# Output projection on normed operands, both parts summed in one bank; three units of up products in step; four reorders

## The chip, the cores and the metric

One core of one Trainium2 chip runs the program. The time is the device time of one execution in microseconds (us); the median of three runs is compared. All matrix products are done in split form: an operand is kept as a high part, rounded to the matmul's format, and a low part, the rest, and a product is three matmuls (high x high, high x low, low x high) into the same bank.

## What is computed

One layer of a hybrid encoder on 1024 tokens of width 1024: a shared norm and input projection, eight heads of attention beside a recurrent block (LRU), an output projection, a gated feed-forward layer of width 2816 with a causal convolution, and a gated addition at the end.

```python
hn = _rms_norm(x, g_mix[l])
proj = hn @ w_in[l]
cq, ckv, kr, xl, gl = jnp.split(proj, IN_SPLITS, axis=-1)
attn = _mla(cq, ckv, kr, positions, ...)
lru = _rglru_block(xl, gl, ...)
mixed = jnp.concatenate([_rms_norm(attn, g_attn_out[l]), _rms_norm(lru, g_lru_out[l])], axis=-1)
x = x + mixed @ w_out[l]
hf = _rms_norm(x, g_ffn[l])
up = _causal_dwconv(hf @ w_up[l], w_ffn_conv[l], b_ffn_conv[l])
gte, val = up[..., :D_FF], up[..., D_FF:]
x = x + (jax.nn.gelu(gte, approximate=True) * val) @ w_down[l]
gate = jax.nn.sigmoid(_rms_norm(x, g_ple[l]) @ w_ple_gate[l] + b_ple_gate[l])
x = x + gate * (p[l] @ w_ple[l])
```

`_rms_norm` divides each token by the root of its mean square and multiplies by a gain per channel.

## The kernel before

Activations lie transposed: 128 channels on the partitions, tokens along the row, in chunks `c` or `k` of 128 channels (eight of them for width 1024) and two halves `h` of 512 tokens. The program is one straight line of instructions. The functions lay down an order, each engine works through its own queue in order, and the tool that builds the program may put a ready instruction ahead of one that waits when it lays the queues down; semaphores are put in for it. DMAs are issued from SyncE's queue (SP), in order too. ScalarE makes high parts, VectorE low parts.

Stages, with their lines:

- `project` (L213) reads x, scales it by the gain, and sums its squares: ScalarE squares a chunk, and the sum over chunks (L255) is on GpSimd for odd chunks up to the fifth and on VectorE otherwise. The first two products run chunk by chunk as x comes in (L262).
- `lru` (L375) goes over four blocks of 128 channels. For each, two gates are computed by small products in the banks `bc` and `st` (L428, L430), then the recurrence; the result y is scaled by its gain, split (L455), and both parts go to DRAM. The sum of the squares of y (`yss`) is on ScalarE, GpSimd or VectorE by block (L460 to L464).
- `qkv` (L551) ends with a dummy Exp (L585) that loads ScalarE's table for the softmax. `attention` (L606) copies two mask rows into the operand buffers of both halves (L629, L633) and then runs jobs in an order by due times, in units of a twelfth of a head: `TURN_AT`, `PROBS_AT`, `BLOCK_AT`, `WEIGH_AT`, and `MIX_AT` for work on the output projection's operands. `mix_attn` (L828) scales a half chunk of the attention output by its gain, splits it, and squares it for the norm; `mix_lru` (L820) fetches the parts of y.
- `mix` (L746) is the output projection. For each half and output chunk, the lru part is summed in one bank and the attention part in another; each bank is multiplied by its norm's scale per token (`rl` and `r1`) and added to the residual `x1` (L773, L774, L786, L787). `measure` (L854) forms the norm's sums over channels on TensorE (L144), `scale` (L858) spreads the scale of each token over all partitions with two matmuls (L164). In the second half, the first operands of the next stage are made (`normed`, `operand`).
- `ffn` (L1019) computes the up products. A unit is 128 gate channels and 128 value channels; its four half-width products are formed from seven (numbered `p`), which need combined operands: B11 and B21 from the first half's residual, T1 to T4 and B22 from both. `T(n, k)` makes them on VectorE and ScalarE, `weights` and `finish_weights` make the combined weights, `product` runs the twelve matmuls, `sums` reads the banks `b1`, `b2`, `b3` into the output tiles `U`, and `finish_unit` (the epilogue, five steps) does convolution, GELU and product into tiles `u`. Units 0 and 1 run in step at the start, then one unit after another. The tiles `U` and `u` (four each) are opened after the residual tiles are closed.
- `down` (L1152) runs two halves of 22 steps of 24 matmuls; after each half `gained` makes the gate's operands and the squares of the new residual, whose sum is on GpSimd. `ple` (L1202) runs the gate's products; the scale of the first half is spread after the second product (n = 1), that of the second after the fifth (n = 4).

Of the kernel before, what the change touches and what calls it, by code (L numbers as in the profile page):

```python
# [47 lines left out]
MIX_AT = (4, 6, 7, 8)  # L48
# [26 lines left out]
class Block:  # L75
# [137 lines left out]
    def project(self):  # L213
# [22 lines left out]
        for k in range(NK):  # L236
# [13 lines left out]
            if k == 0:  # L250
                nc.scalar.activation(ssum, raw, AF.Square)
            else:
                sq = rp.tile([P, S], F32, tag="xsq", name="xsq", bufs=2)
                nc.scalar.activation(sq, raw, AF.Square)
                (nc.gpsimd if k % 2 and k < NK - 1 else nc.vector).tensor_tensor(out=ssum, in0=ssum, in1=sq, op=ALU.add)  # L255
# [119 lines left out]
    def lru(self, x, ws, done, then, scale):  # L375
# [43 lines left out]
        for c in range(NL):  # L419
# [3 lines left out]
            for j, b in ((0, "b_r"), (1, "b_i")):  # L423
                g = slice((2 * c + j) * P, (2 * c + j + 1) * P)
                o = L(b)
                for h in range(2):
# [26 lines left out]

            parts = bx.bitcast(F32R), m.bitcast(F32R)
# [96 lines left out]
    def qkv(self, t, c, uq, ukv):  # L551
# [31 lines left out]
        if t == NT - 1:  # L583

            nc.scalar.activation(tmp, tmp, AF.Exp, scale=0.0)  # L585
# [20 lines left out]
    def attention(self):  # L606
# [12 lines left out]
        self.e = []  # L619
# [6 lines left out]
        mask = self.w.tile([P, S], F32, tag="wraw", name="mask", bufs=3)  # L626
        nc.sync.dma_start(out=mask[QK:QK + NT], in_=self.i["mask"][0])
        for g in range(2):
            nc.scalar.copy(self.qb[g][0][QK:QK + NT], mask[QK:QK + NT, g * HALF:(g + 1) * HALF])  # L629
        mask = self.w.tile([P, S], F32, tag="wraw", name="mask", bufs=3)  # L630
        nc.sync.dma_start(out=mask[QK:QK + NT], in_=self.i["mask"][1])
        for g in range(2):
            nc.scalar.copy(self.kb[g][0][QK:QK + NT], mask[QK:QK + NT])  # L633
# [4 lines left out]
        jobs = []  # L638
# [8 lines left out]
        for at, f, args in zip(MIX_AT, (self.mix_attn, self.mix_attn, self.mix_lru, self.mix_attn), ((0, 0), (1, 0), (0,), (2, 0))):  # L647
# [10 lines left out]
        self.mix_attn(3, 0)  # L658
# [86 lines left out]

    def mix(self):  # L746
        nc = self.nc
        self.banks(at=3, lru=3, bc=1)
        self.c_x1, x1p = self.pool("x1", 1)
# [565 lines left out]
```

## Time and profile before

| what | value |
|---|---|
| median of three runs | 1244.38 us (1241.66 to 1244.45) |
| the profiled execution | 1244.59 us, span 1242.8 us |
| TensorE's mean granted clock | 0.984 |
| TensorE idle within the span | 41.5 us |
| HBM read, written | 97.36 MB, 28.31 MB |

The span is the time from the first to the last instruction of the profiled execution. PE is TensorE (PEld its weight loads), DVE VectorE, ACT ScalarE, POOL GpSimd, SP SyncE. A group of instructions is named by its line, engine, operation and tiles (`out<-in`). A line is often that of a helper: L108 is every chain of matmuls, L113 and L118 the low part of a split, L112 and L117 its high part.

Section 2 of the page cuts the span into forty slices; each digit is the busy share of a slice in tenths (9 is 90% or more), and PEclk is the granted clock in tenths of full speed:

```profile
PE   7999998999999998899999999999999998999998
PEclk9999998999999998899999999999999998999999
```

TensorE is busy nearly everywhere, and where a digit falls the clock's digit beside it often falls too.

### The profile page before, as it was taken

To read this page: it belongs to the slowest core of one execution; us is meant where nothing else is said; L and a number is where in the kernel's file an instruction comes from. 1 tells how busy PE (TensorE), PEld (TensorE's weight loads), DVE (VectorE), ACT (ScalarE), POOL (GpSimd) and SP (SyncE) were. 2 spreads that over 40 slices of the span, in tenths; PEclk is the share of its full clock that TensorE was granted. 3 is DMA by queue.
4 is the path that set the end of the run, shared out by engine and by line. 5 is a ranking of instruction groups with operands and counts; after the bars stand their busy time and mean duration, and the time that the engine had idled before them with its cause. 6 is when DMAs were issued, how large, how long until landed. Compare 5 with 4: busy or idle time off the path is not lost.

```text
span 1242.8 us, 15388 instructions
## 1 busy us (share of the span) xinstructions
PE 1201.3 (97%) x5600; PEld 1001.7 (81%) x5600; DVE 896.6 (72%) x1406; ACT 643.6 (52%) x1030; POOL 165.8 (13%) x180
## 2 busy tenths in 40 slices
PE   7999998999999998899999999999999998999998
PEld 5787986888878887788888888888888886888787
DVE  7879798777778699998878878778653346444633
ACT  7388677888874134654544545545432244333211
POOL 3012264444430000000000000000000021001200
PEclk9999998999999998899999999999999998999999
DMA  6213200111168220322222222122485336641221
GB/s 226 68 55 111 103 7 9 48 36 55 43 196 291 86 73 22 107 97 85 85 85 85 69 102 85 68 88 86 132 286 186 106 103 219 202 153 51 69 101 69
DMA packets 49932, 128.78 MB, mean 104 GB/s; under 512 B 5808, under 2 KB 8752, under 8 KB 49856
## 3 DMA queue, kind: packets, MB, share of 16 engines
q1 hardware_dynamic: 49856, 127.80, 30.2%
q8 instruction: 44, 0.72, 0.2%
q14 instruction: 32, 0.26, 0.1%
HBM read 97.36 MB, written 28.31 MB: 101 GB/s over the span
## 4 chain that ended last, share of the span: by engine, by line
PE 66%; DVE 6%; issue 1%; DMA 0%; ACT 0%; POOL 0%; POOLq 0%; DVEq 0%
PE b L108 31%; PE dn L108 16%; PE gt L108 6%; PE lru L108 4%; PE at L108 3%; PE st L108 2%; DVE m L118 1%; DVE B L911 1%; PE big L108 1%; DVE x L1038 1%; DVE x L1177 1%; DVE x L896 0%; PE p L734 0%; PE st L144 0%; DMA om<-oc 0%
## 5 line engine op out<-in xcount | busy, mean ns | idle before, releaser
L108 PE MATMUL b<-B,A 128*128 128x512 f32 x1848 | 424.9, 392 | 3.7 <-DVE U L992 3.4
L108 PEld LDWEIGHTS b<-B,A 128*128 128x128 f32 x1848 | 349.7, 190 | 78.0 <-issue 3.8
L108 PE MATMUL dn<-m,whi 128*128 128x512 f32 x616 | 191.9, 392 | 4.9 <-DVE m L113 4.9
L113 DVE TENSOR_TENSOR wlo<-wraw,whi 128x1024 fp32r<-128x1024 f32 (+2 forms) x59 | 68.1, 1157 | 123.8 <-ACT whi L112 123.8
L108 PEld LDWEIGHTS dn<-m,whi 128*128 128x128 f32 x616 | 116.8, 190 | 29.9 <-DVE m L113 5.4
L112 ACT CAST whi<-wraw 128x1024 fp32r<-128x1024 f32 (+2 forms) x59 | 58.4, 994 | 147.0 <-PE st L108 136.7
L108 PE MATMUL dn<-m,wlo 128*128 128x512 f32 x308 | 120.9, 392 | 0.0
L1004 DVE SCALAR_TENSOR_TENSOR u<-U,par,u 128x1023 f32<-128x1023 f32 x88 | 112.4, 1278 | 2.1 <-ACT u L1009 2.0
L846 POOL TENSOR_TENSOR ssum<-ssum,sq 128x512 f32<-128x512 f32 x14 | 21.4, 1532 | 658.7 <-ACT sq L842 657.9
L944 ACT CAST A<-s 128x512 fp32r<-128x512 f32 x88 | 54.7, 622 | 78.0 <-PE b L108 70.8
L108 PE MATMUL gt<-m,wh 128*128 128x512 f32 (+1 forms) x272 | 80.0, 377 | 0.0
L108 PE MATMUL big<-kT,qT 96*128 96x384 f32 (+11 forms) x288 | 68.7, 365 | 3.5 <-ACT kT L117 3.3
L952 DVE TENSOR_TENSOR A<-s,A 128x512 fp32r<-128x512 f32 x88 | 60.6, 689 | 14.7 <-ACT A L944 14.6
L108 PEld LDWEIGHTS dn<-m,wlo 128*128 128x128 f32 x308 | 58.5, 190 | 12.1
L972 ACT COPY keep<-b 128x512 f32<-128x512 f32 x66 | 38.4, 583 | 52.4 <-PE b L108 52.4
L702 DVE TENSOR_SCALAR_CACHE_REDUCE pr<-big,nrq 128x512 f32<-128x512 f32 (+3 forms) x64 | 51.9, 814 | 11.7 <-PE p L715 4.3
L706 POOL TENSOR_SCALAR pr<-pr,st 128x512 f32<-128x512 f32 (+3 forms) x64 | 48.2, 757 | 78.5 <-DVE st L705 59.9
L944 ACT CAST A<-wraw 128x512 fp32r<-128x512 f32 x54 | 33.4, 622 | 47.8 <-PE b L108 40.5
L108 PEld LDWEIGHTS big<-kT,qT 96*128 96x128 f32 (+1 forms) x288 | 50.3, 198 | 9.1 <-ACT kT L117 3.8
L108 PEld LDWEIGHTS gt<-m,wh 128*128 128x128 f32 x272 | 50.0, 188 | 9.3
L1009 ACT ACTIVATE u<-U,par 128x1024 f32<-128x1024 f32 x44 | 54.7, 1246 | 1.5 <-DVE U L994 0.4
L704 ACT ACTIVATE pr<-pr,st 128x512 f32<-128x512 f32 (+3 forms) x64 | 49.7, 777 | 8.0 <-DVE pr L702 6.8
(327 smaller groups left out, 2289.8 us busy)
## 6 DMA issues: line engine op xcount, KB each, us to landing
wraw<-w_down SPq DMA_DIRECT2D x44, 512.0 KB, 3.4
wraw<-w_up SPq DMA_DIRECT2D x33, 512.0 KB, 3.3
g<-u SPq DMA_DIRECT2D x22, 512.0 KB, 2.6
graw<-g SPq DMA_DIRECT2D x44, 256.0 KB, 4.1
raw<-w_up SPq DMA_DIRECT2D x11, 512.0 KB, 3.4
e<-eo SPq DMA_DIRECT2D x16, 256.0 KB, 2.4
m<-y SPq DMA_DIRECT2D x8, 512.0 KB, 7.2
x<-xT SPq DMA_DIRECT2D x16, 256.0 KB, 7.0
```

Of the source, the lines that this page charges most:

```text
L108: self.nc.tensor.matmul(out, lhsT=w, rhs=x, start=start and n == 0, stop=stop and n == len(terms) - 1, **kw)
L112: self.nc.scalar.copy(hi, src)
L113: (self.nc.gpsimd if pool else self.nc.vector).tensor_tensor(out=lo, in0=src, in1=hi.bitcast(F32), op=ALU.subtract)
L702: V.tensor_scalar(out=pv, in0=sc, scalar1=self.nrq[:, qt, h:h + 1], scalar2=None, op0=ALU.mult, op1=ALU.min, accum_out=st[:, 0:1])
L704: nc.scalar.activation(pv, pv, AF.Exp, bias=st[:, 0:1], scale=-1.0, accum_out=st[:, 1:2])
L706: nc.gpsimd.tensor_scalar(out=pr[:, :kend], in0=pr[:, :kend], scalar1=st[:, 2:3], scalar2=1.0, op0=ALU.mult, op1=ALU.mult)
L846: (nc.gpsimd if pool else nc.vector).tensor_tensor(out=self.ssum[key], in0=self.ssum[key], in1=sq, op=ALU.add)
L944: self.nc.scalar.copy(t[:, :HALF], src)
L952: self.nc.vector.tensor_tensor(out=lo, in0=src, in1=hi.bitcast(F32), op=ALU.subtract)
L972: self.nc.scalar.copy(t, self.bank[u, b])
L1004: tap = lambda z, d: V.scalar_tensor_tensor(out=self.u[u, z][:, d:], in0=self.U[u, z][:, :S - d], scalar=self.col(f"cw{2 - d}", z * NF + u ...
L1009: nc.scalar.activation(t, self.U[u, n], AF.Identity, bias=self.col("cb", n * NF + u), scale=self.col("cw2", n * NF + u))
```

## The change

In the output projection, the operands are normed before the matmuls. `scale_lru` spreads the lru norm's scale once, during the last head; `mix_lru` fetches y (now one tile, not two parts), multiplies it by gain and scale and splits it; `mix_attn` multiplies the attention output by gain and scale, after `measure` and `scale` of the attention norm, and splits it. The squares are a job of their own (`square_attn`). Both parts of a chunk are summed in one bank of seven; the order of parts in the first half is written out. One addition reads the bank into the residual.

The residual's sixteen half tiles are laid in eight whole ones with the tags `U` and `u`, which the up products' output tiles take over without the pool being closed. Units 0, 1 and 2 of the up products run in step at the start (units 0 and 1 before); T4 is made later; the raw weights rotate through five places in the order of w_up.

Reorders and smaller edits: all of the input's sums of squares on VectorE; the last block's second gate in one wide bank, with one Sigmoid; the sum of squares of y by ScalarE squares and VectorE additions; the dummy Exp and the second half's mask copies after the first two turns of head 0; the first half's `gained` spread over steps 1 to 8 of the down product's second half; the gate's scales spread after n = 2 and n = 5.

```diff
-                (nc.gpsimd if k % 2 and k < NK - 1 else nc.vector).tensor_tensor(out=ssum, in0=ssum, in1=sq, op=ALU.add)
+                nc.vector.tensor_tensor(out=ssum, in0=ssum, in1=sq, op=ALU.add)
...
+                if c == NL - 1 and j:
+                    ps = self.acc("big")
+                    for h in range(2):
+                        hs = slice(h * HALF, (h + 1) * HALF)
+                        self.chain(ps[:, hs], self.three(gw, (xch, xcl), (slice(None), g), (slice(None), hs)))
+                    nc.scalar.activation(o, ps, AF.Sigmoid, bias=self.col(b, c))
...
-            self.scaled(y, self.col("g_lru", c), *parts)
-            self.y.append(self.dr.tile([P, 2, S], F32, name=f"y{c}"))
-            for j, z in enumerate((bx, m)):
-                nc.sync.dma_start(out=self.y[c][:, j, :], in_=z)
+            self.y.append(self.dr.tile([P, S], F32, name=f"y{c}"))
+            nc.sync.dma_start(out=self.y[c], in_=y)
...
-                e = V if c == NL - 1 else nc.gpsimd
-                e.tensor_tensor(out=gl, in0=y, in1=y, op=ALU.mult)
-                e.tensor_tensor(out=self.yss, in0=self.yss, in1=gl, op=ALU.add)
+                nc.scalar.activation(gl, y, AF.Square)
+                V.tensor_tensor(out=self.yss, in0=self.yss, in1=gl, op=ALU.add)
...
-            nc.scalar.activation(tmp, tmp, AF.Exp, scale=0.0)
...
+        hide(0)
...
+        jobs = [(TURN_AT[0] + .1, tables, ()), (TURN_AT[0] + .2, hide, (1,))]
...
+        for at, f, args in zip(MIX_AT, (self.scale_lru, self.square_attn, self.square_attn, self.mix_lru, self.square_attn),
+                               ((), (0, 0), (1, 0), (0,), (2, 0))):
...
+        def lru(h, c):
+            ps[h, c] = self.acc("mx")
+            self.chain(ps[h, c], [z for k in range(NL, NK) for z in self.three(
+                ws[c], mx[k][h], (slice(None), slice(k * P, (k + 1) * P)), slice(None))], stop=False, skip_group_check=True)
+        def attn(h, c):
+            hs = slice(h * HALF, (h + 1) * HALF)
+            o, x = ps.pop((h, c)), self.x1[c][h]
+            self.chain(o, [z for k in range(NL) for z in self.three(
+                ws[c], mx[k][h], (slice(None), slice(k * P, (k + 1) * P)), slice(None))], start=False, skip_group_check=True)
+            V.tensor_tensor(out=x, in0=o, in1=x, op=ALU.add)
+            nc.sync.dma_start(out=self.xs[c][:, hs], in_=x)
+            self.square(("x1", h), c, x)
...
+        lru(0, 0)
+        self.square_attn(3, 0)
+        residual(0)
+        lru(0, 1)
+        self.measure("at", 0, NL * P)
+        lru(0, 2)
+        operands(0)
+        self.load_wout(range(WOUT_EARLY, NK))
+        lru(0, 3)
+        for k in range(NL):
+            self.square_attn(k, 1)
+        lru(0, 4)
+        attn(0, 0)
+        lru(0, 5)
+        self.mix_lru(1)
+        attn(0, 1)
...
+        for c in range(NK):
+            lru(1, c)
...
+            attn(1, c)
...
-            V.tensor_tensor(out=ps, in0=ps, in1=rl[h], op=ALU.mult)
-            V.tensor_tensor(out=self.x1[c][h], in0=ps, in1=self.x1[c][h], op=ALU.add)
...
-            V.tensor_tensor(out=o, in0=o, in1=self.r1[:, hs], op=ALU.mult)
-            V.tensor_tensor(out=x, in0=o, in1=x, op=ALU.add)
...
     def mix_lru(self, h):
...
+            self.nc.vector.scalar_tensor_tensor(out=y, in0=y, scalar=self.col("g_lru", c), in1=self.rl[:, hs],
+                                                op0=ALU.mult, op1=ALU.mult)
+            self.mx[NL + c][h] = self.pair(h)
+            self.split(y, *self.mx[NL + c][h])
...
-        self.order = [(0, 1), (0, 2), (1, 1), (1, 2), (2, 1)] + [(u, p) for p in (5, 6, 7, 3, 4) for u in range(2)]
+        self.order = ([(u, p) for u in range(3) for p in (1, 2)] + [(u, p) for p in (5, 6, 7, 3) for u in range(2)]
+                      + [(2, p) for p in (5, 6, 7, 3)] + [(u, 4) for u in range(3)])
...
-            self.U[u, z] = self.fp.tile([P, S], F32, tag=f"U{z}", name=f"U{z}", bufs=2)
+            self.U[u, z] = self.xp.tile([P, S], F32, tag="U", name=f"U{z}", bufs=NL)
...
+                if h and 1 <= j <= NK:
+                    self.gained(j - 1, 0, "g_ple", "x2", pool=True)
...
-            if n in (1, 4):
+            if n in (2, 5):
                 self.scale("x2", n // 3)
```

More of the change, by code (lines that the diff above doesn't have):

```diff
@@ L425, in lru @@
                 o = L(b)
-                for h in range(2):
+                if c == NL - 1 and j:
[4 more added lines that the diff above has]
+                    nc.scalar.activation(o, ps, AF.Sigmoid, bias=self.col(b, c))
+                for h in range(2 if c < NL - 1 or not j else 0):
                     hs = slice(h * HALF, (h + 1) * HALF)
@@ L618, in attention @@
         self.pp = [self.wload(self.i["pT"][k]) for k in range(2)]
-        self.e = []
+        self.e = [self.dr.tile([P, S], F32, name=f"e{c}") for c in range(NK)]
         self.tp = tp
@@ L625, in attention, with hide, tables @@
         self.kb = [[tp.tile([QK + NT * (j == 0), S], F32R, name=f"kT{j}{g}") for j in range(2)] for g in range(2)]
[L626 to L633, printed above, removed]
+        mask = [self.w.tile([P, S], F32, tag="wraw", name="mask", bufs=3) for _ in range(2)]
+        for j in range(2):
+            nc.sync.dma_start(out=mask[j][QK:QK + NT], in_=self.i["mask"][j])
+        def hide(g):
+            nc.scalar.copy(self.qb[g][0][QK:QK + NT], mask[0][QK:QK + NT, g * HALF:(g + 1) * HALF])
+            nc.scalar.copy(self.kb[g][0][QK:QK + NT], mask[1][QK:QK + NT])
+        def tables():
+            t = self.nv.tile([P, 2, H], F32, tag="htmp", name="tab", bufs=2)
+            nc.scalar.activation(t[:, 0, :], self.mhalf[:, :H], AF.Exp)
+        hide(0)
         self.kT, self.qT = {}, {}
@@ new lines, in residual, with operands @@
+        def residual(h):
+            for k in range(NK):
+                nc.sync.dma_start(out=self.x1[k][h], in_=self.i["xT"][k][:, h * HALF:(h + 1) * HALF])
+        def operands(h):
+            self.scale("at", h)
+            for k in range(NL):
+                self.mix_attn(k, h)
+        lru(0, 0)
[6 more added lines that the diff above has]
+        self.load_wout(range(WOUT_EARLY, NK))
@@ new lines, in mix @@
+        lru(0, 3)
+        for k in range(NL):
+            self.square_attn(k, 1)
+        lru(0, 4)
+        attn(0, 0)
+        lru(0, 5)
+        self.mix_lru(1)
+        attn(0, 1)
+        lru(0, 6)
+        attn(0, 2)
+        self.measure("at", 1, NL * P)
+        lru(0, 7)
+        attn(0, 3)
+        operands(1)
+        residual(1)
+        for c in range(4, NK):
+            attn(0, c)
+        for c in range(NK):
+            lru(1, c)
+            if c == 0:
+                self.measure("x1", 0, D)
+            if c == 1:
+                self.scale("x1", 0)
+                for n in range(3):
+                    self.fetch()
+            attn(1, c)
+            for k in {1: (0,), 2: (1, 2), 3: (3,), 4: (4, 5), 5: (6,), 6: (7,)}.get(c, ()):
+                self.normed(k, 0)
+                self.operand(("B21" if k >= NL else "B11", k % NL), self.x1[k][0], self.m[0])
+                self.finish_operand()
+            if 3 <= c < 7:
+                self.weights(c - 3)
+                self.finish_weights(c - 3)
@@ L1122, in ffn @@
             self.sums(u, p)
-            if (u, p) == (1, 7):
-                for z in range(2):
-                    self.sums(z, 2)
+            if i in (13, 14):
+                for k in range(2 * (i - 13), 2 * (i - 13) + 2):
+                    T(4, k)
+                self.finish_operand()
             if self.epilogue and (p not in (2, 3) or len(self.epilogue) > 5):
@@ L1177, in down @@
                         V.tensor_tensor(out=self.x1[c][h], in0=ps[c], in1=self.x1[c][h], op=ALU.add)
-            for c in range(NK):
-                self.gained(c, h, "g_ple", "x2", pool=True)
+        for c in range(NK):
+            self.gained(c, 1, "g_ple", "x2", pool=True)
         self.c_ff = cg
```

211 lines of the change are left out of this document (85 added, 126 removed).

## The prediction

> **What bounds the kernel now.** I read the page's first part, then for whom TensorE waited, then a table by stage, and only then the instructions around each wait.
>
> ```profile
> PE 1201.3 (97%) x5600; PEld 1001.7 (81%) x5600; DVE 896.6 (72%) x1406; ACT 643.6 (52%) x1030; POOL 165.8 (13%) x180
> ```
> ```profile
> PE dn L108 <- DVE m L113: 4.9, 1, 4.9
> PE big L262 <- DVE xl L118: 4.7, 4, 2.2
> PE st L144 <- DVE ssum L846: 3.8, 1, 3.8
> PE b L108 <- DVE U L992: 3.4, 1, 3.4
> PE big L108 <- ACT kT L117: 3.3, 1, 3.3
> PE bc L108 <- ACT b_r L430: 2.8, 1, 2.8
> ```
> ```profile
> PE st L734 <- ACT ph L112: 1.7, 1, 1.7
> PE st L164 <- DVE dg L162: 1.3, 1, 1.3
> ```
> ```profile
> 198.00:214.00 16.00, 12.53 (x54) 10.19 (x53) 10.99 (x31) 11.00 (x25) 4.14 (x9) 0.79 0.05 17
> 364.00:376.00 12.00, 9.87 (x42) 7.48 (x41) 9.08 (x11) 7.24 (x12) 2.59 (x2) 0.86 0.78 259
> 376.00:464.00 88.00, 88.00 (x400) 72.75 (x399) 71.09 (x117) 26.97 (x42) 3.41 (x3) 1.00 0.40 143
> 464.00:480.00 16.00, 12.19 (x47) 9.84 (x46) 14.46 (x27) 4.93 (x9) 1.01 (x1) 0.79 0.23 81
> 480.00:520.00 40.00, 36.31 (x147) 28.84 (x146) 40.00 (x66) 23.68 (x40) 0.00 (x0) 0.91 0.16 53
> 1028.00:1042.00 14.00, 9.07 (x29) 6.96 (x29) 10.50 (x13) 4.04 (x6) 1.04 (x1) 0.76 0.66 208
> ```
> TensorE is the bound: 1201.3 of 1242.8 us. The change takes no matmul away (the projection keeps its two halves of eight chunks of 24), so what can be won is the 41.5 us of idle time, and something behind each stall: the granted clock. In a wait row stand total, times and longest; in a table row the stretch, its length, the busy time (and count) of PE, PEld, DVE, ACT and POOL, the clock, the DMA share and GB/s. A clock of 0.79 over 16 us is 2 x 0.21 x 16 = 6.7 us at half speed; row 364 gives 3.4 us. So a stall costs its idle time and then half of the work's time at half speed: up to 1.7 us after a short one (364), up to 3.4 after a long one (198, 464, 480, 1028). Where part of the slow stretch is idle itself, I take 2.7 to 2.9 for the latter. Together that is far more than the idle time alone, and the four places where VectorE is named hold the most of it.
>
> **Part by part**, gains negative.
>
> *Input squares (L255), from GpSimd to VectorE.*
>
> ```profile
> L255 DVE TENSOR_TENSOR yss<-yss,xsq x4: 1218/1221/1223, 17.9 to 33.1; 128x1024 f32<-128x1024 f32 x4
> ```
> ```profile
> L255 POOL TENSOR_TENSOR yss<-yss,xsq x3: 2623/3305/3328, 12.1 to 25.5; 128x1024 f32<-128x1024 f32 x3
> ```
> ```profile
> 12.13 2.62 POOL L255 TENSOR_TENSOR yss<-yss,xsq 128x1024 f32<-128x1024 f32 x1 [7.81 <-ACT xsq L254]
> ```
> ```profile
> 12.40 2.37 DVE L366 TENSOR_TENSOR lacc<-lacc,s 128x4 f32<-128x4 f32 x1
> ```
> While GpSimd adds, VectorE is held: an operation on 4 columns lasts 2.37 us. Three such holds of about 2.2 us go, three adds of 1.22 come: 6.6 - 3.7 = 2.9 of VectorE's time, on which all four L262 waits (4.7) hang. Bounds -4.7 and -1; taken **-2.8**, and later the split of the next weights is VectorE's to deliver, so not all four waits go.
>
> *Last gate in one wide bank, running sum of y on ScalarE.* The 2.8 us wait on b_r is that of the third block's second gate, to whose r ScalarE comes late; only the fourth block's second gate is changed, and TensorE has the next stage's matmuls behind that. The scaling of y leaves ScalarE and VectorE, a square comes on ScalarE at the same place, waiting for the same y. Taken **-0.3**; bounds -4.2 (wait and a short clock stretch gone) and +1.
>
> *Start of attention.*
>
> ```profile
> 196.21 1.13 ACT L629 CAST qT<-mask 8x512 fp32r<-8x512 f32 x2
> ```
> ```profile
> 197.25 1.04 ACT L633 CAST kT<-mask 8x1024 fp32r<-8x1024 f32 x1
> ```
> ```profile
> 199.61 1.28 ACT L585 ACT_TABLE_LOAD   x1
> ```
> TensorE waits 3.3 us for kT (L117), which stands in ScalarE's order behind four mask copies and the table load for Exp. Half of the copies (0.6 + 1.0) and the load (1.3) go behind it: 2.9. The first Exp waits for the first scores and VectorE's pass over them, which hides the load there. With 0.4 us of stall left, one of the two half-speed windows in row 198 should go (1.6). Taken **-4.5**; bounds -6.3 and -1.5. The second mask's DMA is only issued earlier.
>
> *Tail of attention.* ScalarE stops for the half of `at` that comes by DMA (the 1.7 us wait on ph, then the short slow stretch); a square now stands where the scaling stood and waits for the same. The last head gets the first four lru operands and two spreads and loses scalings of about the same number. Taken **0**; bounds -3.8 and +2.
>
> *Output projection.*
>
> ```profile
> L773 DVE TENSOR_TENSOR lru<-lru,rl 128x512 f32<-128x512 f32 x16 | 11.1, 695 | 1.9 <-PE lru L108 1.9
> L786 DVE TENSOR_TENSOR at<-at,r 128x512 f32<-128x512 f32 x16 | 10.9, 693 | 3.5 <-PE at L108 2.1 <-ACT r L860 1.4
> L774 DVE TENSOR_TENSOR x<-lru,x 128x512 f32<-128x512 f32 x16 | 10.9, 686 | 0.1
> L787 DVE TENSOR_TENSOR x<-at,x 128x512 f32<-128x512 f32 x16 | 10.9, 684 | 0.1
> ```
> ```profile
> L118 DVE SCALAR_TENSOR_TENSOR m<-at,par,m 128x512 fp32r<-128x512 f32 x5 | 3.6, 747 | 2.4 <-ACT m L117 2.4
> ```
> Per chunk four VectorE operations become one: 43.8 - 10.9 = 33 us less. Eight lru operands (0.75 + 0.68 = 1.43 each, the first four still in attention) and one subtraction more for each of eight attention operands (0.68) come: 17. Net 16 us, and row 376 shows that none of it is in TensorE's way there: it pays later. What is new is that the attention part waits for the norm.
>
> ```profile
> 387.50 2.72 PE at L108 x12
> ```
> ```profile
> 371.25 0.69 DVE L846 TENSOR_TENSOR ssum<-ssum,sq 128x512 f32<-128x512 f32 x1
> ```
> ```profile
> 383.67 0.95 PE L144 MATMUL st<-ones,ssum 128*128 128x1 f32 x8
> ```
> ```profile
> 391.19 0.59 ACT L860 COPY r<-st 128x512 f32<-128x512 f32 x1 [5.90 <-PE st L164]
> ```
> From statistics to scale took 8.1 us; four operands then need 4 x 1.43 on VectorE, which also splits w_out. In program order the statistics follow two lru groups (2 x 2.72), the first attention group five (13.6): 5.4 + 8.1 + 5.7 = 19.2, up to 5.6 late, 7.3 with a short slow stretch. But the sum of squares was ready at 371.9, so the statistics can run before those groups; then nothing is late. Bounds 0 and +7.3; taken **+3** between them (1.3 idle, 1.7 clock). Behind the waiting matmul stand the other lru groups, if their w_out is there: on SyncE's queue the residual's eight loads now stand ahead of w_out's last three, as before.
>
> By the Trainium skill ("TensorE: Matmul & The Clock Gate", Part 1: The HAM clock gate) the array falls to half rate after at least one idle window of about 3.4 us. The stretches of 3.4 and 6.7 us agree with the length of that window, but in row 364 a wait of 1.7 us was enough, so the rows decide; by the page this stall would cost its idle time alone and the sum would be 1.7 us lower.
>
> *Start of the up products.* Its two large waits (3.8 and 3.4) and two slow stretches (2.9 and 2.8) cost 12.9 now.
>
> ```profile
> 480.37 1.20 DVE x L1038 x2
> 481.57 0.66 DVE x L896
> ```
> ```profile
> 492.17 1.20 DVE B L911 x2
> ```
> ```profile
> L1004 DVE SCALAR_TENSOR_TENSOR u<-U,par,u 128x1023 f32<-128x1023 f32 x88 | 112.4, 1278 | 2.1 <-ACT u L1009 2.0
> ```
> ```profile
> L1009 ACT ACTIVATE u<-U,par 128x1024 f32<-128x1024 f32 x44 | 54.7, 1246 | 1.5 <-DVE U L994 0.4
> ```
> The first wait is VectorE's backlog from the projection; with 16 us less it goes, and its slow stretch (6.7 together). Then VectorE works without a gap (40.00 of 40.00), and the wait on U comes at the end of that. The chain gives 0.60 and 0.66 from start to start. Needed by the thirteenth product: T1 and T2, 4 x 1.86 each; T3, 4 x 1.2; B22, 4 x 0.6; thirteen weight operations of 0.6: 30 us. They start when the scale is there, one product (2.7) and the 8.1 of above after TensorE's first: they end at 41. TensorE has six products that need finished operands alone, not five, and reaches the end of the thirteenth's operands at 12 x 2.72 + 2 = 34.7. Late 6.1, in pieces below 2 us, so no clock. The order also wants six U tiles in four places: the second unit's sum waits for the first unit's Identity and two taps (1.25 + 2 x 1.28), which can run early, but on a full VectorE: 1.5. So 12.9 becomes 7.6: taken **-5.3**; bounds -12.9 and +3. The later epilogues hide behind products of 2.72 each, one step of about 1.3 beside each.
>
> *Turn of the down product.*
>
> ```profile
> L118 DVE SCALAR_TENSOR_TENSOR m<-x,par,m 128x512 fp32r<-128x512 f32 x8 | 10.6, 1390 | 0.0
> ```
> ```profile
> L113 DVE TENSOR_TENSOR wl<-wraw,wh 128x1024 fp32r<-128x1024 f32 x1 | 1.2, 1211 | 0.0
> ```
> These eight, slowed to 1.39 by GpSimd's adds beside them, stand ahead of the splits for which TensorE waits 4.9, and then has the clock (2.7). They move to steps 1 to 8 of the second half, one in 24 matmuls (5.4 us), where two wide splits and a narrow one (1.2 + 1.2 + 0.7) leave room even in odd steps. Taken **-7.2**; bounds -7.6 and -6.
>
> *Gate scale one step later.* The 1.3 us wait on dg gets 5.4 us of cover more. Taken **-1.3**; bounds -1.4 and 0.
>
> Sum: -2.8 - 0.3 - 4.5 + 0 + 3 - 5.3 - 7.2 - 1.3 = -18.4. The profiled execution took 1244.59 (span 1242.8, 1.8 around it), the median of the runs is 1244.38, so the same: 1244.6 - 18.4 = **1226.2**.
>
> **The rivals.**
>
> *Every stall of the middle goes.* For: 16 us of VectorE are freed just ahead of where it is late. Then 0 instead of +3, -12.9 instead of -5.3, and about half of what the first three parts can give more (5): 1226.2 - 15.6 = 1210.6. Against: T1 to B22 are not fewer. 20%.
>
> *The norm chain is late in full:* the 7.3 instead of 3, and 2 for late w_out: 1232.5. For: VectorE splits w_out just then. Against: its other load there falls. 18%.
>
> *It gives back what it won:* +7.3 at the projection, nothing at the up products, -1.5 at attention's start: 1239. 9%.
>
> *Slower: four places for six U tiles.* If the epilogues aren't run ahead, the fourth product of the second, third and fourth unit each waits for a chain of copy, Identity, two taps and sum: 0.6 + 1.25 + 2.56 + 0.7 and the steps between, about 6, and 2.7 of clock: three cost 26, so 1252. It decides from 22 us of such waits (slower by over 0.3%), that is from the third. For: in row 480 VectorE has no gap to run them ahead. Against: other units' matmuls can stand between, and the waits are known when the order is made. 8%.
>
> **How the numbers follow.** Forecast 45% (1219 to 1233), the rivals 20, 18, 9 and 8. The range 1208 to 1240 leaves out the last, half of the third and a little of the first. 0.3%, about what a measurement of this kernel can tell from no change, is 3.7 us, up to 1240.6. Faster: 45 + 20 + 18 and 2 of the third's 9, 85%; same 7%; slower 8%.
>
> **What would show it.** Right: the waits of `dn` on m and of `st` on dg gone, no clock below 1 around the down product's turn; kT's wait under 1 us; one add per projected chunk on VectorE; VectorE full after the norm of the new residual, with small waits of `b` on B. Wrong: a wait over 4 us at the projection's first attention group; waits of `b` behind U sums or taps in products 19 to 30; waits of L262 as before. The doubt is greatest where the order laid down at compile time meets real durations, in these two places.

## The result, and the profile after

| what | before | after |
|---|---|---|
| median of the runs compared (four each) | 1243.13 us | 1222.40 us (1218.71 to 1223.14) |
| the profiled execution | 1244.59 us, span 1242.8 | 1222.06 us, span 1219.9 |
| TensorE's mean granted clock | 0.984 | 0.994 |

The ratio is 0.9828, with a 95% interval of 0.9803 to 0.9852: faster by 1.7%. The prediction was 1226.2 us, 3.8 us above the median. Forecast was a gain of 18.4 us; the medians moved by 20.7 and the spans of the two profiled executions by 22.9. That it came so near is partly chance: its terms were off by up to 6 us, in both directions.

The first part of the page of after, busy time of each engine and its share of the span:

```profile
PE 1192.3 (98%) x5600; PEld 994.8 (82%) x5600; DVE 872.4 (72%) x1382; ACT 645.7 (53%) x1035; POOL 145.9 (12%) x173
```

TensorE runs the same 5600 matmuls, in 9.0 us less (less time at half clock), and is idle for 27.6 us instead of 41.5. Now for whom it waits (total, times, longest, in us), after:

```profile
PE t L325 <- DVE cqkv L317: 3.8, 2, 3.1
PE bc L108 <- ACT b_r L437: 2.7, 1, 2.7
...
PE dn L108 <- DVE wlo L113: 2.0, 1, 2.0
...
PE big L108 <- DVE pr L707: 1.4, 2, 1.2
PE mx L108 <- DVE wlo L113: 1.4, 1, 1.4
PE p L682 <- DVE qT L113: 1.1, 1, 1.1
...
PE big L262 <- DVE xl L118: 0.5, 1, 0.5
...
PE st L164 <- DVE dg L162: 0.4, 1, 0.4
PE b L108 <- DVE A L1007: 0.4, 1, 0.4
...
PE p L682 <- DVE kT L118: 0.2, 1, 0.2
...
```

Four of the six large waits of before are gone or below 0.6 us: those of L262, of `st` on the sum of squares, of `b` on U, and of the scores on kT. The wait on b_r stayed. The down product still waits, now for wlo, 2.0 us instead of 4.9. The wait on cqkv was 0.7 us before and is new in its size: no part of the prediction has it. The waits on pr and on qT (1.1 us) are new too.

The table by stage of after (length, busy time of PE, PEld, DVE, ACT and POOL with counts, clock, DMA share, GB/s):

```profile
124.00:132.00 8.00, 7.31 (x33) 7.01 (x34) 4.08 (x8) 6.98 (x10) 0.00 (x0) 0.79 0.00 0
198.00:214.00 16.00, 14.23 (x73) 11.52 (x73) 13.41 (x40) 12.78 (x30) 5.92 (x9) 0.89 0.04 16
364.00:376.00 12.00, 10.41 (x48) 8.46 (x49) 9.31 (x14) 7.50 (x11) 2.93 (x2) 1.00 0.83 267
458.00:480.00 22.00, 22.00 (x102) 18.14 (x101) 19.80 (x35) 10.24 (x18) 1.32 (x1) 1.00 0.07 25
480.00:520.00 40.00, 39.31 (x168) 30.43 (x167) 39.80 (x64) 24.47 (x40) 0.00 (x0) 1.00 0.28 92
1008.00:1024.00 16.00, 13.97 (x55) 11.11 (x54) 15.09 (x14) 8.49 (x12) 5.85 (x4) 0.89 0.56 185
```

The start of the up products (458 to 520) has no slow clock left and 0.69 us idle. The start of attention and the turn of the down product each keep a wait and half the slow time. The first row is the new loss, behind the wait on cqkv.

Where the time went is best read from the start of each stage's first matmul. Lengths in us, each the difference of two such starts in the profiled execution of that kernel (the last to the end of the span); the columns run to the product after the first two (`big<-xh,wh`, number 2 in the expectations, counted from 0), from there to the first q product, from there to the first projection product, and so on. The lower kernels are the experiments below:

| kernel | to product 2 | recurrence, columns | attention | projection | up | down | gate |
|---|---|---|---|---|---|---|---|
| before | 36.9 | 128.2 | 205.1 | 94.1 | 435.2 | 246.0 | 97.3 |
| after | 32.6 | 129.8 | 202.1 | 94.1 | 423.8 | 242.4 | 95.1 |
| input squares on GpSimd | 36.9 | 132.7 | 200.9 | 95.7 | 423.8 | 239.6 | 95.0 |
| y squares on GpSimd | 32.5 | 134.4 | 203.4 | 94.1 | 423.8 | 242.4 | 95.0 |
| sum of part 2 put off | 32.4 | 130.0 | 202.1 | 94.1 | 423.8 | 240.8 | 95.1 |
| half banks | 31.8 | 124.5 | 200.7 | 95.7 | 423.8 | 239.6 | 95.1 |
| half banks, y squares on GpSimd | 32.6 | 129.8 | 203.5 | 94.1 | 423.8 | 242.3 | 95.0 |
| masks first | 32.7 | 129.1 | 201.4 | 94.8 | 423.8 | 240.8 | 95.1 |
| Exp first | 33.2 | 128.0 | 203.6 | 94.1 | 423.8 | 242.4 | 95.1 |
| down as before | 32.6 | 130.1 | 202.1 | 94.6 | 423.8 | 245.9 | 95.0 |
| down sums on VectorE | 32.5 | 130.3 | 202.1 | 95.8 | 423.8 | 238.5 | 95.1 |
| VectorE loaded | 32.8 | 129.8 | 202.1 | 99.7 | 425.7 | 240.8 | 95.1 |
| two units in step | 33.0 | 129.0 | 203.6 | 94.1 | 428.4 | 239.6 | 94.9 |
| half banks, down sums on VectorE | 32.6 | 125.3 | 200.7 | 95.7 | 423.8 | 238.5 | 95.1 |

From before to after the stages give -4.3, +1.7, -3.0, 0, -11.4, -3.6 and -2.2: -22.9 of the span. Half of it is the up products' start.

How far a stage moves without an edit in it can be read from the same table. The recurrence took 128.0 to 130.3 us in the kernels that have its code and its operands of after, attention 200.7 to 203.6, the projection 94.1 to 95.8, the down products 239.6 to 242.4; the up products took 423.8 each time. (For each stage, kernels with an edit in it, or just ahead of it, are left out.)

### The profile page after: what moved, and what is told of

Its sections match the earlier page's. It is cut to its first block, busy times and chain, and to the rows that moved or that the text cites. A ratio compares the mean times of both kernels' runs of the same rounds, so it can differ in the third digit from the quotient of the medians.

```text
span 1219.9 us, 15336 instructions
## 1 busy us (share of the span) xinstructions
PE 1192.3 (98%) x5600; PEld 994.8 (82%) x5600; DVE 872.4 (72%) x1382; ACT 645.7 (53%) x1035; POOL 145.9 (12%) x173
## 4 chain that ended last, share of the span: by engine, by line
PE 71%; DVE 5%; ACT 0%; issue 0%; POOL 0%; DVEq 0%; ACTq 0%; POOLq 0%
PE b L108 32%; PE dn L108 17%; PE gt L108 7%; PE mx L108 7%; PE st L108 3%; PE big L108 2%; PE p L739 1%; PE p L720 1%; DVE B L965 1%; DVE x L1088 1%; PE p L108 1%; DVE x L950 0%; PE st L720 0%; PE st L144 0%; DVE m L113 0%; DVE A L1007 0%
## 5 line engine op out<-in xcount | busy, mean ns | idle before, releaser
L108 PE MATMUL b<-B,A 128*128 128x512 f32 x1824 | 416.1, 390 | 0.7 <-DVE A L1007 0.4
L108 PEld LDWEIGHTS b<-B,A 128*128 128x128 f32 x1824 | 341.6, 188 | 74.2 <-DVE A L1007 1.1
L108 PEld LDWEIGHTS dn<-m,whi 128*128 128x128 f32 x616 | 116.5, 189 | 24.2
L108 PE MATMUL mx<-m,woh 128*128 128x512 f32 x192 | 59.4, 391 | 0.0
```

Source lines behind the costliest of these rows:

```text
L108: self.nc.tensor.matmul(out, lhsT=w, rhs=x, start=start and n == 0, stop=stop and n == len(terms) - 1, **kw)
```

## The experiments

Each kernel is the changed one with the edit shown; times are medians of four executions (five for the last), to be held against 1222.4 us (0.9803 to 0.9852), with the interval of the ratio to the kernel before.

**The input's sums of squares back on GpSimd.**

```diff
-                nc.vector.tensor_tensor(out=ssum, in0=ssum, in1=sq, op=ALU.add)
+                (nc.gpsimd if k % 2 and k < NK - 1 else nc.vector).tensor_tensor(out=ssum, in0=ssum, in1=sq, op=ALU.add)
```

> The changed kernel (1222.4 us) with the three sums of squares at the start (L255) back on GpSimd. Theory, the prediction's first step: VectorE's operand pieces wait for GpSimd's adds again, product 2 starts 2.8 to 4.3 us later than 32.59 us and the slow stretch at 40 to 44 us returns, 1.7 us more; first group of the 416 columns near 121 us instead of 115.95, whole time 1226 to 1228 us. Rival: the recurrence behind it is limited by its own chain and takes the loss up; first group of the 416 columns within 1 us of 115.95, whole time 1222 us.

Measured 1228.5 us (0.9871 to 0.9912). Product 2 starts at 36.94 us instead of 32.59, and the waits of L262 are 4.0 us instead of 0.5 (4.7 before). The edit is worth what the theory says at its own place. The rival, that the recurrence behind it takes the loss up, is wrong: it takes 2.9 us longer itself. Why is not shown.

**The wait on cqkv.** My reading of after was that the sum of squares of y, now on VectorE behind a ScalarE square, stands ahead of cqkv. VectorE's timeline in after (start, length, instruction, in brackets the idle time before it and what ended it):

```profile
118.20 3.46 DVE L459 TENSOR_TENSOR y<-m,gl 128x1024 f32<-128x1024 f32 x1
122.79 1.23 DVE L466 TENSOR_TENSOR yss<-yss,gl 128x1024 f32<-128x1024 f32 x1 [1.12 <-ACT gl L465]
123.93 0.61 DVE L317 TENSOR_SCALAR cqkv<-a,rx 128x384 f32<-128x384 f32 x1
```

and GpSimd's beside it:

```profile
118.17 2.41 POOL L447 TENSOR_TENSOR b_i<-b_i,xc 128x1024 f32<-128x1024 f32 x1 [10.90 <-DVE m L457]
```

Three kernels were to tell this from the other edit there, the wide bank. The squares of parts 1 and 2 back on GpSimd:

```diff
-                nc.scalar.activation(gl, y, AF.Square)
-                V.tensor_tensor(out=self.yss, in0=self.yss, in1=gl, op=ALU.add)
+                e = V if c == NL - 1 else nc.gpsimd
+                e.tensor_tensor(out=gl, in0=y, in1=y, op=ALU.mult)
+                e.tensor_tensor(out=self.yss, in0=self.yss, in1=gl, op=ALU.add)
```

> The changed kernel with the squares of y of parts 1 and 2 back on GpSimd (two instructions each), part 3 on VectorE, as before. Theory: the wait of 3.09 us of the first transposes for cqkv is made by the sum of squares that now stands ahead of it on VectorE and itself waits for ScalarE's square; it falls below 1 us, the slow stretch at 124 to 132 us goes with it, the first q product starts 3 to 4.5 us earlier than 162.41 us, whole time 1218 to 1219.5 us. Rival: the last gate's wide bank made the wait by moving the work of the parts against each other; then the wait stays at 2.5 to 3.5 us and the time at 1222 us.

The sum of part 2 put off:

```diff
+            elif c < NL - 1:
+                nc.scalar.activation(gl, y, AF.Square)
+                kept = gl if c == NL - 2 else V.tensor_tensor(out=self.yss, in0=self.yss, in1=gl, op=ALU.add)
             else:
+                V.tensor_tensor(out=self.yss, in0=self.yss, in1=kept, op=ALU.add)
                 nc.scalar.activation(gl, y, AF.Square)
```

> The changed kernel with ScalarE's squares kept, but the sum of part 2 issued with that of part 3, behind its y. Theory: as with the squares on GpSimd, but without GpSimd's adds beside VectorE: the transposes' wait falls below 1 us and the time to 1217.5 to 1219.5 us. Rival of the wide bank: wait and time as in the changed kernel, 1222 us. Third: y itself lasted 3.46 us instead of 1.22 because GpSimd's product ran beside it, so cqkv ends near 122.4 us even so and a wait of 0.6 to 1 us stays, with a time of 1219 to 1220 us.

The last gate in half banks:

```diff
-                if c == NL - 1 and j:
-                    ps = self.acc("big")
...
-                for h in range(2 if c < NL - 1 or not j else 0):
+                for h in range(2):
```

> The changed kernel with the last gate's second bank back in two half banks. Theory that the sum of squares makes the wait for cqkv: the wait stays at 2.5 to 3.5 us, the matmuls wait for the half banks again (2.7 us in the changed kernel in all), time 1222 to 1224 us. Rival: the wide bank made the wait; it falls below 1 us, time 1218 to 1220 us.

Measured: 1226.3 us (0.9850 to 0.9883) with the squares on GpSimd, 1222.3 (0.9821 to 0.9855) with the sum put off, and 1215.3 (0.9764 to 0.9799) with half banks. My theory fell: it had the wait below 1 us with the squares on GpSimd, and unchanged with half banks. With the squares on GpSimd the transposes wait longer still:

```profile
PE t L325 <- DVE cqkv L317: 5.0, 3, 3.9
```

and with half banks hardly at all:

```profile
PE t L325 <- DVE cqkv L317: 0.7, 1, 0.7
```

The kernel with the sum put off says nothing, since the order laid down when the program is built put the sum at its old place again (at 122.72 us, ahead of cqkv). With half banks VectorE's timeline is

```profile
116.87 1.23 DVE L452 TENSOR_TENSOR y<-m,gl 128x1024 f32<-128x1024 f32 x1
119.30 0.62 DVE L317 TENSOR_SCALAR cqkv<-a,rx 128x384 f32<-128x384 f32 x1 [1.21 <-PE a L108]
```

and GpSimd's product of the last block comes 3.7 us later:

```profile
121.85 2.40 POOL L440 TENSOR_TENSOR b_i<-b_i,xc 128x1024 f32<-128x1024 f32 x1 [15.90 <-ACT b_i L430]
```

The wide bank lets the last gate's single Sigmoid run early (it ends at 118.10 us; the second of the two with half banks ends at 121.77). So GpSimd's product meets y, which lasts 3.46 us instead of 1.23; the sum then has its place ahead of cqkv. That the bank is the cause of the wait is shown. By the timelines y is 2.2 us longer, and the sum with its idle time puts cqkv off by 2.3 more; neither was tried by itself. In the whole stage half banks leave TensorE 4.1 us idle instead of 6.7, and no slow stretch instead of two.

**Both edits of the recurrence as before**, to see the squares alone (the two diffs above together).

> The changed kernel with the recurrence as before in both its edits: half banks for the last gate, and the squares of y of parts 1 and 2 on GpSimd. Beside the run with half banks alone (1215.3 us) it shows the squares by themselves. Theory, the prediction's: the squares on ScalarE save what GpSimd's four instructions cost their neighbours on VectorE, 1 to 4 us (with the wide bank it was 3.9 us); time 1217 to 1219.5 us. Rival: ScalarE's square makes VectorE wait, and GpSimd is the better place when the half banks are there; 1213 to 1215 us.

Measured 1221.1 us (0.9805 to 0.9848). The direction is the theory's, and the saving is larger than its 1 to 4 us: 5.8 us between the two kernels with half banks. Its reason is not what the rows show. Without the ScalarE squares TensorE waits here:

```profile
PE bc L108 <- ACT xch L112: 4.2, 2, 4.0
```

What comes late is the next block's xc, and VectorE stood idle for it:

```profile
105.10 0.69 ACT L430 ACTIVATE b_i<-st,par 128x512 f32<-128x512 f32 x1
105.69 1.24 ACT L404 ACTIVATE xc<-u,par 128x1024 f32<-128x1024 f32 x1
```
```profile
106.95 2.41 DVE L406 SCALAR_TENSOR_TENSOR xc<-u,par,xc 128x1023 f32<-128x1023 f32 x1 [5.40 <-ACT xc L404]
```

Between the two halves of the gate b_i, ScalarE's order here has a table load, an Exp and a second table load (101.34 to 105.09 us). With half banks alone it does not have them there, and xc starts at 103.37. The kernel before, which has neither edit of the recurrence, does not have them there either. The first of xc's three steps on VectorE then meets GpSimd's product of b_i as well, and lasts 2.41 us. So the undo changed the order laid down, and what GpSimd's four instructions cost their neighbours is not shown apart from that.

In the stage from product 2 to the first q product the four kernels make a table that closes: wide bank 129.8 us with ScalarE's squares and 134.4 with GpSimd's, half banks 124.5 and 129.8. As these kernels were built the squares win about 5 us, the wide bank loses about 5 us, and the two edits together give 0.0, to within the some 2 us by which the stage moves by itself.

**The start of attention.** First an undo that did not restore the executed order:

```diff
-        hide(0)
+        hide(0)
+        hide(1)
...
-        jobs = [(TURN_AT[0] + .1, tables, ()), (TURN_AT[0] + .2, hide, (1,))]
+        jobs = []
...
+        if t == NT - 1:
+            nc.scalar.activation(tmp, tmp, AF.Exp, scale=0.0)
```

> The changed kernel with the attention's start as before: the Exp that loads the table behind the last token's scales, and all six mask copies ahead of the first turns. Theory, the prediction's step: the first scores wait for kT again, 2.9 to 4.5 us with the slow stretch, whole time 1225 to 1227 us. Rival: since the measured gain from the first q product to the first operand of the output projection was only 3.05 us in all, half of it came from elsewhere; then the time is 1223 to 1224 us.

Measured 1221.0 us (0.9802 to 0.9850), the same as after. The masks ran first, but ScalarE had the table load at 198.34 us behind three of the operands, so this shows only that all four mask copies first, with the load behind some operands, cost nothing in all. The next kernel has masks and table load ahead of the operands, as before:

```diff
-        jobs = [(TURN_AT[0] + .1, tables, ()), (TURN_AT[0] + .2, hide, (1,))]
+        jobs = [(TURN_AT[1] - .1, hide, (1,)), (TURN_AT[1] - .05, tables, ())]
```

> The changed kernel with the four mask copies and the Exp table ahead of the first turned operands on ScalarE, the executed order of before (the earlier run on this had put the Exp behind three of the operands). Prediction's step: the wait of 3.35 us for kT is back with its slow stretch, first scores 2.9 to 4.5 us later, time 1225 to 1227 us. Rival: what is lost at the first scores is taken up later in the attention, whose second half is set by other waits; time 1222 to 1223 us.

Measured 1223.2 us (0.9822 to 0.9863). The wait for kT is back as it was:

```profile
PE big L108 <- ACT kT L117: 3.5, 1, 3.5
```

but attention as a whole takes only 1.5 us more than in after (203.6 against 202.1), as the rival had it. In after, most of the time that kT no longer takes is taken by smaller waits, on qT (1.1 in the first turns) and pr (1.4): in the first 60 us TensorE is idle for 4.8 us, against 5.4 with Exp first. A slow stretch follows in both, of 3.4 us in after and of 6.8 with Exp first. With Exp first:

```profile
200.00:204.00 4.00, 4.00 (x16) 3.54 (x15) 2.36 (x11) 2.34 (x7) 0.78 (x2) 0.50 0.18 66
```

In after:

```profile
204.00:208.00 4.00, 4.00 (x14) 3.19 (x14) 2.85 (x6) 2.17 (x7) 1.83 (x4) 0.57 0.00 0
```

So what is shown is 0.6 us of idle time. The rest of the 1.5 is the clock, and it can't be put down to the edit: two kernels with the attention of after took 203.5 and 203.6 us as well, and two others 200.7.

**The start of the up products: freed VectorE or new order.** First VectorE's time taken away again, where the change had freed it (48 instructions more; their results are not used):

```diff
             self.square(("x1", h), c, x)
+            for _ in range(3):
+                V.tensor_tensor(out=o, in0=o, in1=x, op=ALU.max)
```

> The changed kernel with three further VectorE instructions of 128x512 behind each of the sixteen projected chunks, 33 us of VectorE's time, about what the change took off it there; their results are not used. Theory: the start of the up products lost its 12 us of waits because VectorE has time at the end of the projection to prepare their operands; then VectorE is busy throughout 440 to 460 us, the first up products wait 5 to 9 us again, and the time is 1228 to 1233 us. Rival: the order in step of three units removed the waits; then the first down product moves by less than 2 us and the time is 1222 to 1224.5 us.

Measured 1227.4 us (0.9853 to 0.9887); the first down product starts at 890.08 us instead of 882.41, 7.7 later, which is in the theory's direction; the wait and the time are a little under its range. The wait for the sum of squares, 3.8 us before and absent in after, is back:

```profile
PE st L144 <- DVE ssum L890: 4.2, 1, 4.2
```

The end of the projection, in the loaded kernel,

```profile
440.00:460.00 20.00, 18.85 (x84) 15.29 (x82) 20.00 (x34) 6.02 (x10) 0.00 (x0) 1.00 0.15 54
```

and in after,

```profile
440.00:460.00 20.00, 20.00 (x90) 16.57 (x89) 5.36 (x9) 2.83 (x5) 0.00 (x0) 1.00 0.11 40
```

shows VectorE full and nearly idle: 20.00 and 5.36 us of 20. Over the whole projection VectorE was busy for 77.2 us before, 64.4 in after and 92.9 with the load, so the load is more than had been freed, and its price an upper bound. Then the old order with VectorE free (lines that follow from it are left out here):

```diff
-        self.order = ([(u, p) for u in range(3) for p in (1, 2)] + [(u, p) for p in (5, 6, 7, 3) for u in range(2)]
-                      + [(2, p) for p in (5, 6, 7, 3)] + [(u, 4) for u in range(3)])
+        self.order = ([(0, 1), (0, 2), (1, 1), (1, 2), (2, 1)] + [(u, p) for p in (5, 6, 7, 3, 4) for u in range(2)]
+                      + [(2, p) for p in (5, 6, 2, 7, 3, 4)])
...
-            if i in (13, 14):
+            if i in (11, 12):
```

> The changed kernel with the up products at the start in the old order: two units in step, then unit 2 by itself (its first product early, as before); the new places of the tiles and the freed VectorE time stay. Theory from the run with added VectorE work (7.5 of the 11.4 us came back with the load): the order and what it lets follow are worth the other 3.9 us; the first up products wait for a sum or an operand 2 to 4 us in all, first down product near 886 us instead of 882.4, time 1225 to 1228 us. Rival: with VectorE free ahead of them either order is fed in time; first down product within 1 us, time 1222 us.

Measured 1224.9 us (0.9834 to 0.9876); the up stage takes 4.5 us more than in after, where it is the same in every kernel with the same code, and waits are there:

```profile
PE b L108 <- DVE U L1047: 1.5, 1, 1.5
PE b L108 <- DVE B L965: 0.9, 2, 0.5
PE b L108 <- ACT B L957: 0.7, 2, 0.5
```

TensorE is idle for 3.4 us of the stage instead of 0.7; the other 1.8 us are in longer matmuls, and why is not shown. Both halves matter: up to 7.5 us for the freed VectorE (5.6 ahead of the first up product, 1.9 behind), 4.5 us for the order, against 11.4 gained in all. What the tiles' new places give by themselves was not tried.

**The turn of the down product.** The loop behind the first half, as before:

```diff
-                if h and 1 <= j <= NK:
-                    self.gained(j - 1, 0, "g_ple", "x2", pool=True)
...
+            for c in range(NK):
+                self.gained(c, h, "g_ple", "x2", pool=True)
```

> The changed kernel with the eight squares and operands of the first half's residual in one loop behind the half, as before, instead of one at each step of the second half. Prediction's step: the waits of the turn come back whole, 7.2 us, time 1229.6 us. As measured between the two kernels: the stage from the first down product to the first gate product shrank by 3.6 us only; time 1226 us. Rival: the new wait of 2.0 us there is made by the spreading itself and cancels it; time 1222 us.

The spread squares, but summed on VectorE:

```diff
-                    self.gained(j - 1, 0, "g_ple", "x2", pool=True)
+                    self.gained(j - 1, 0, "g_ple", "x2")
```

> The changed kernel with the first half's sums of squares in the down stage on VectorE instead of GpSimd. Theory: GpSimd's adds hold VectorE's operations beside them (the m pieces take 1.78 us instead of 0.68, wl 2.31 instead of 1.21), and this makes the matmuls' wait of 2.0 us for wlo and the slow stretch behind it; without them the wait falls below 0.5 us, first gate product 2 to 4 us earlier than 1124.82 us, time 1218.5 to 1220.5 us. Rival: VectorE is full there by its own work, and seven adds more of 0.68 us make the wait longer; time 1222 to 1225 us.

Measured 1226.3 us (0.9846 to 0.9878) and 1218.1 us (0.9769 to 0.9812). The undo costs the 3.5 us that the traces gave, with the old wait of 4.9 us. In kernels with the down products of after the stage took 239.6 to 242.4 us, against 246.0 before: a gain of 3.6 to 6.4, and the prediction's 7.2 in none. With the sums on VectorE TensorE waits nowhere at the turn:

```profile
1016.00:1020.00 4.00, 4.00 (x19) 3.34 (x18) 4.00 (x7) 2.17 (x4) 0.00 (x0) 1.00 0.76 251
```

VectorE is full there in both. But in after it is held by GpSimd's adds,

```profile
1011.94 2.31 DVE L113 TENSOR_TENSOR wl<-wraw,wh 128x1024 fp32r<-128x1024 f32 x1
...
1017.80 2.29 DVE L113 TENSOR_TENSOR wlo<-wraw,whi 128x1024 fp32r<-128x1024 f32 x1
```
```profile
1017.36 1.64 POOL L888 TENSOR_TENSOR ssum<-ssum,sq 128x512 f32<-128x512 f32 x1 [1.96 <-ACT sq L884]
```

while with all seven adds in its own queue the same splits take

```profile
1011.40 1.22 DVE L113 TENSOR_TENSOR wl<-wraw,wh 128x1024 fp32r<-128x1024 f32 x1
```

Seven adds of 0.68 us on VectorE cost it less than seven adds of GpSimd beside it. Of the 3.9 us that the stage wins, 2.0 are the wait, and the slow stretch behind it is nearly all the rest.

**The two finds together**: half banks, and the down sums on VectorE.

> Two edits to the changed kernel together: half banks for the last gate again, and the first half's sums of squares in the down stage on VectorE. Theory: the stalls lie in different stages, so the gains add up, 7.1 and 4.3 us; 1210 to 1212.5 us. Rival: one of them was in part the measured runs' spread; 1213 to 1216 us.

Measured 1213.4 us (0.9745 to 0.9789): the lowest median, but not certainly below half banks alone (1215.3), and the rival's figure, not the theory's. The gains do not add up: with half banks alone the down stage, whose code is the same as in after, took 239.6 us already and not 242.4 (a wait of 0.8 us instead of 2.0, and no slow stretch), so 1.1 us was left of the 3.9. Two other kernels with the down products of after took 239.6 us too, so this is not the half banks' doing. Why the wait is shorter there stays open.

## Why the prediction was near, point by point

- **Input squares**, -2.8. At the next product the gain is 4.3: nearly all of the L262 waits went (4.7 to 0.5), where I had expected that "not all four waits go". By the first q product 2.7 of it is left in the kernel with both recurrence edits undone (162.34 us; before 165.05). The direction was right; the size is less sure, for in that kernel y's scaling and split are gone as well, and in the changed kernel the undo costs 6.1, beyond the bound of 4.7.
- **Last gate and sum of y**, -0.3. The sum is right (0.0) by luck, and its reasons are wrong. I wrote that TensorE has the next stage's matmuls behind that gate and that a square "comes on ScalarE at the same place". With the squares on GpSimd the kernels were 5 us slower, with a ScalarE order that makes the next block late; the wide bank lost 5, because an earlier Sigmoid moved GpSimd's product beside y. Neither was looked for.
- **Start of attention**, -4.5. Measured -1.9 to the 101st score matmul (85.6 us behind the first q product instead of 87.5), and 1.5 by the undo. That kT's wait goes to 0.2 us was right; what came next late was not named. The step that failed is "with 0.4 us of stall left": 2.5 us of waits on qT and pr took the place. One of the two half-speed windows did go in after (row 198 to 214: clock 0.89 instead of 0.79), but with the same attention none, one or two are left, by the kernel.
- **Tail of attention**, 0. The wait on ph went from 1.7 us to 0.3, and from the 101st score matmul on the stage is 1.1 us shorter (116.5 against 117.6), inside the bounds.
- **Output projection**, +3. Measured 0. The chain was sized well: statistics 7.2 us after the first product (371.68 against 364.50), three of the four operands ready at 382.7 and the last, held back on VectorE, at 386.2. But "the first attention group five" groups in took a group as one block. In the built order the matmuls of attention (weights whi, wlo of chunk 0) and lru groups (woh, wol) alternate from 384 us on, so each takes what is ready: 0.4 us of wait, that of `st` on dg.

```profile
384.57 0.50 PE L108 MATMUL mx<-m,wol 128*128 128x512 f32 x1
384.91 0.40 PE L108 MATMUL mx<-m,whi 128*128 128x512 f32 x1
385.15 0.63 PE L108 MATMUL mx<-m,woh 128*128 128x512 f32 x2
```

A wait of 1.4 for the split of the weights is new, and the slow stretch at the stage's start (0.86 in row 364) is absent. So the 0 is itself a balance: in the kernels that have the projection of after and a slow stretch the stage took 95.7 us, 1.6 more than before.
- **Start of the up products**, -5.3. Measured -11.4, near the first rival's -12.9. The first wait went as argued. The step that failed is "late 6.1". The operands started 10.5 us after the first product (at 458.59), as I had it, but the last were done 37 us after it and not 41. VectorE's timeline of after, from the first combined weights over the norm (L950) to the last of B22:

```profile
459.99 0.69 DVE L984 TENSOR_TENSOR s<-wraw 128x512 f32<-128x512 f32 x1
...
467.98 0.68 DVE L990 TENSOR_TENSOR s<-wraw,raw 128x512 f32<-128x512 f32 x1
469.14 1.41 DVE L950 SCALAR_TENSOR_TENSOR x<-x,par,r 128x512 f32<-128x512 f32 x2 [0.48 <-ACT r L902]
...
494.32 1.28 DVE L965 TENSOR_TENSOR B<-x,B 128x512 fp32r<-128x512 f32 x2
```

VectorE made six combined weights while the norm's scale was on its way; I had counted them all behind it. (The kernel before made six there as well, from 468.44 us on.) That covers 4 of the 6.1. Most of the rest is on TensorE's side: its thirteenth product started 35.2 us after the first and not 12 x 2.72 = 32.6, because the norm's own matmuls (0.9 and 0.5 us) and small waits for weights (0.4 and 0.2 us) lie between. I also left the order's own share (4.5) out, and priced its places at 1.5, for which no wait came.
- **Turn of the down product**, -7.2. Measured -3.6, and up to -6.4 in kernels with the same down products. The sign named beforehand, no clock below 1 around the turn, did not come: 0.57 behind 1020 us. I had moved the squares out of the splits' way, but took GpSimd's adds along without asking what they would hold in the second half: the rule I had read for L255 (VectorE is held while GpSimd adds) applied here and I did not use it.
- **Gate scale**, -1.3. From the two traces -2.2; the wait of 1.3 us is gone. No slow stretch had stood behind it (clock 1.00 from 1157 to 1169 us before), so where the other 0.9 comes from is not shown. This was not tried by itself.

Of the rivals, the first was right about the up products and the projection, and wrong in the 5 us more that it gave the first three parts (1210.6 in all); the slower one (six U tiles in four places) did not occur: no wait of `b` on U is left in after. The terms sum to -18.4 against -22.9 in the span; the errors of the attention's start and the down turn (6.2, too hopeful) and of the projection and the up products (9.1, too cautious) largely cancel.

## What to carry to other kernels

Ask of each edit which instruction it makes earlier, and what that one will then run beside: a gate that finished early cost about 5 us, in idle time and slow clock together, because GpSimd's product then ran into VectorE's critical work. A sum moved between GpSimd and VectorE is priced by what it does to the neighbours, not by its own length; and an undo can change the order of other engines too, so read their timelines before naming the cause. And undo edits one at a time even when the whole is a gain: here a good change was 7 us better without one of its parts.

## What the hardware showed beside that

The same wait does not always cost the clock. At the down turn, after and the first attention undo have the same code; in after

```profile
1020.15 0.75 PE L108 MATMUL dn<-m,wlo 128*128 128x512 f32 x1 [2.03 <-DVE wlo L113]
```

the clock falls at 1020.23 us:

```profile
1016.82:1020.23 3.41, 1.38 (x7) 0.84 (x5) 3.41 (x4) 1.97 (x3) 1.64 (x1) 1.00 0.72 255
1020.23:1023.64 3.41, 3.41 (x8) 2.69 (x9) 2.86 (x4) 0.62 (x1) 0.00 (x0) 0.50 0.67 226
```

and in the other, behind a wait of the same length,

```profile
1019.59 0.50 PE L108 MATMUL dn<-m,wlo 128*128 128x512 f32 x1 [2.02 <-DVE wlo L113]
```

it stays full:

```profile
1014.73:1018.14 3.41, 2.84 (x13) 2.02 (x11) 3.41 (x5) 0.64 (x1) 1.45 (x2) 1.00 0.93 310
1018.14:1021.56 3.42, 1.97 (x9) 1.62 (x10) 3.42 (x4) 2.09 (x3) 0.31 (x1) 1.00 0.51 156
```

That is the 1.6 us between their down stages (242.4 and 240.8). The rows are laid on a grid that the traces show. The slow stretches of after, but for one at its end, start at 102.04, 125.94, 204.44 and 1020.23 us, which are 7, 23 and 239 times 3.413 us apart, and each lasts 3.41; in all fourteen traces the slow stretches lie on such a grid, at another offset in each, and last 3.41 or 6.83 us (but for the last one of a trace, at its end). In after the wait of 2.03 us lies in one window of the grid; in the other kernel a border splits it into 0.57 and 1.45. Counted over all traces (from 25 us on, without the last 5), each of the 32 full-speed windows with 1.9 us of idle time or more was followed by a slow one; of the 57 with 1.0 to 1.9, 12 were, and what decides among those is not shown. So for a wait of some 2 us its place on the grid decides whether it costs the clock.

In the table of stages the projection takes mostly 94.1 or 95.7 us, and attention 200.7, 202.1 or 203.5, in kernels whose edits lie elsewhere: steps of about 1.5 us, each a slow stretch more or less. The two profiled executions of after and of half banks differ by 8.9 us in span (7.1 in the medians); 5.3 of that are at the edit's place, and the rest is largely such stretches elsewhere. Differences of two kernels below some 3 us are not to be put down to an edit without a look at the clock of the stages it does not touch.

The Trainium skill ("TensorE: Matmul & The Clock Gate", Part 1: The HAM clock gate) says that the window in which activity is watched runs freely, whatever the kernel does; the grid agrees with that, in its step of 3.413 us and in its offset, which differs from trace to trace. That by the same section of the Trainium skill a whole idle window of about 3.4 us is needed does not agree: 2.03 us was enough here.
